# A two-layer decoder trunk: Strassen units copy their first product earlier and place plain pieces later, new costs for the ordering estimate, stores moved to the scalar engine

## The chip, the cores and the metric

The kernel runs on one core of a Trainium2 chip. Its engines are TensorE (PE in the rows; PEld is its weight load), VectorE (DVE), ScalarE (ACT), GpSimd (POOL) and SyncE (SP, which issues DMAs). The metric is the device time of one execution in microseconds (us).

## The reference

`reference()` computes a decoder trunk over 512 tokens of 2048 features. Layer 0 runs an RG-LRU recurrence beside sliding-window attention, layer 1 multi-head latent attention (MLA) beside differential attention. What of it the change touches:

```python
def layer(x):                       # both layers, cut
    z = rmsnorm(x) @ w_in           # one input projection, columns shared out among all branches
    yA, yB = branchA(zA), branchB(zB)
    y = concat(yA * silu(gateA), yB * silu(gateB))
    return x + y @ w_out
# layer 1, branch A: MLA, 8 heads, causal softmax over 512 keys
# layer 1, branch B: differential attention, 8 heads, softmax(q1 k1) - lambda * softmax(q2 k2)
out = rmsnorm(layer1(layer0(x)))
```

## The kernel before

**Products.** Matrices are float32, and a product is made of three products of a reduced type (fp32r): every operand is split into a high half (ACT copies it with rounding) and a low half (DVE subtracts), and PE adds high by high, low by high and high by low. Tiles are named by what they hold: `wr` and `wx` raw weights, `wh` and `wl` their halves, `sh`/`sl`, `yh`/`yl`, `th`/`tl` halves of activations; `mm`, `o`, `sc` and `pt` are the PSUM banks, two of each name.

**Weights.** They come in pieces of 128 x 1024. SP loads a piece, ACT writes its high half and DVE its low one, two pieces ahead of PE (`Piece.want`). There are three slots for the halves: those of piece i may be written only when PE has ended piece i-3. A `Sum` is a piece that DVE first adds up from others.

**Order.** `Plan` is a list scheduler that works while the program is built: the order of PE's, ACT's and DVE's instructions is fixed by its estimates. `pe_cost`, `act_cost` and `dve_cost` say how long an instruction takes, `HOP` is what passes from one engine to another, and generators that `yield after(tile)` go on once the estimate has that tile ready. The order on POOL and SP comes from a scheduler behind it. All instructions are issued through one helper, so that every row of the trace carries its line, L62, and is told by its tiles.

**The two units.** Near the end of layer 1's input projection, `Unit` makes two blocks of 1024 columns in a Strassen-like way: over halves of tokens and features, seven products in place of eight, and sums of products in place of the rest. Its banks are X (`mm`), Y (`o`) and Z (`sc`). X takes the first product (pieces p1), Y and Z the next two (p5, p6); then `first` copies X into two tiles s1 (ACT), and DVE makes s2 = Z + s1 and s3 = Y + s2. The pieces T3_0 to T3_2 go on in X, and the plain pieces P_0 and P_1, products of features outside the scheme, begin anew in Z and Y, which `second` hands over when s3 is planned as done. A T3 or p piece is 12 matmuls of 512 columns, a plain piece 24. The trace shows s1, s2 and s3 as `s`.

```python
def steps(self, name, *ops):          # combine, leave, free: generators, one for each of two banks
    def f():
        for b in range(2):
            for op in ops:
                yield from op(b)
```

**Stores.** When a unit's sums are ready, `away` scales them on ACT and stores them to scratch memory (`vd` and `gd`, eight each); five MLA gates are stored so too (`mgd`). POOL issues these stores.

**End of the layer-1 attention.** Each MLA head makes scores (`sc`), a maximum on DVE with a copy to `p`, an exponential on ACT, a scaling on DVE, transposes on PE (`pt<-p`), a copy on ACT (`aT<-pt`), products with the values on PE (`o<-aT,v`), DVE's product with the gate (`mg<-o,mg`), and the halves `yh` (ACT) and `yl` (DVE), which the output projection reads. Heads run in pairs, and matmuls of the output projection lie between their steps.

Of the kernel before, what the change touches and what calls it, by code (L numbers as in the profile page):

```python
# [15 lines left out]
P = 128  # L16
# [50 lines left out]
def _free(ap):  # L67
    n = 1
    for d in ap.shape[1:]:
        n *= d  # L70
    return n


class Plan:
# [40 lines left out]
    def pe_cost(self, op, args, kw):  # L115
        if op == "transpose":
            return 0.108
        rhs = args[2]
        n = _free(rhs)
        if rhs.dtype == F32R:  # L120
            return 0.003 + (n / 2400.0 if n >= 256 else 0.213)
        return 0.006 + max(n, 64) * 4 / 2400.0

    TABLES = {AF.Exp: "e", AF.Sigmoid: "s", AF.Sqrt: "q", AF.Silu: "u"}

    def act_cost(self, op, args, kw):
        c = 0.1 + _free(args[1]) / 1200.0
        if "accum_out" in kw:
            c += 0.09
        t = self.TABLES.get(args[2])  # L130
        if args[2] == AF.Tanh and self.table not in ("e", "s", "u"):
            t = "s"
        if t and t != self.table:
            self.table = t
            c += 1.3
        return c
# [20 lines left out]
    def after(self, *aps):  # L157

        return max(self.ready.get(a.tensor.name, 0.0) for a in aps)
# [33 lines left out]
def trunk_kernel(ctx: ExitStack, tc, xT, w0, w0o, wg, w1, w1u, wuq, wuk, wuv, w1o, small, cst, outT, outN):  # L193
# [3 lines left out]
    act = Engine(plan, "ACT", nc.scalar, plan.act_cost)  # L197
    dve = Engine(plan, "DVE", nc.vector, plan.dve_cost)
    pool = Engine(plan, "Pool", nc.gpsimd, plan.dma_cost)
    sync = Engine(plan, "SP", nc.sync, plan.dma_cost)  # L200
    after = plan.after
# [17 lines left out]
    def wk(name, dt=F32):  # L219
        return bp.tile([P, S], dt, name=nm(name), tag="w")[:, :]  # L220
# [10 lines left out]
    def bank(tag):  # L231

        t = min(banks[tag])
        banks[tag].remove(t)
        plan.now = max(plan.now, t)
        return ps.tile([P, S], F32, name=nm(tag), tag=tag, bufs=2)[:, :]
# [46 lines left out]
    class Piece:  # L283
# [4 lines left out]
        def __init__(self, src, n, kept=False):  # L288
            self.src, self.n, self.kept = src, n, kept
            self.i = len(pieces)  # L290
            pieces.append(self)
# [150 lines left out]
    def big_job(wt, m, X, done, pre=None, norm=None, kept=(False, False), tag="mm"):  # L442
        return Job(big_parts(wt, m, kept), X, done, pre, norm, tag)
# [92 lines left out]
    first = [bank("o"), bank("o")]  # L536
    W, raws, xin = {}, {}, [None] * KT
# [25 lines left out]
    for k in range(KT):  # L563
# [8 lines left out]
        c = slice((k % 4) * P, (k % 4 + 1) * P)  # L572
# [55 lines left out]
    def evac(acc, norm, name):  # L628
        z = wk(name)
        dve.tensor_tensor(z, acc, norm.r, ALU.mult)  # L630
        return z
# [454 lines left out]
    mgd = dp.tile([8, P, S], F32, name="mgd")[:, :, :]  # L1086
# [3 lines left out]
    def mla_gate_job(h, away):  # L1090
        def done(acc):
            z = evac(acc, n1, "mg")

            def f():
                yield after(z)
                act.activation(z, z, AF.Silu)
                if away:
                    yield after(z)
                    pool.dma_start(mgd[h], z)
                else:  # L1100
                    MG[h] = z
            plan.spawn(f())
        j = big_job(w1, 16 + h, X1, done, None, n1)
        if h == 0:
            j.pre = lambda: plan.spawn(differences())
# [5 lines left out]
    def differences():  # L1111

        A, B = slice(0, 256), slice(256, 512)

        def fetch(k):
            xa, xb = wk("xa"), wk("xb")
            sync.dma_start(xa, x1d[k])
            sync.dma_start(xb, x1d[8 + k])
            return xa, xb

        nxt = fetch(0)
        for k in range(NT):
            xa, xb = nxt
            if k + 1 < NT:
                nxt = fetch(k + 1)
            yield after(xa, xb)
            act.activation(xa, xa, AF.Identity, scale=col(C_G1 + k))
            act.activation(xb, xb, AF.Identity, scale=col(C_G1 + 8 + k))
            yield after(xa, xb)
            t13, t42 = wk("ta"), wk("tb")  # L1130
            dve.tensor_tensor(t13[:, A], xa[:, A], xa[:, B], ALU.subtract)
            dve.tensor_tensor(t42[:, A], xb[:, A], xb[:, B], ALU.subtract)
            dve.tensor_tensor(t13[:, B], xa[:, B], xb[:, B], ALU.subtract)
            dve.tensor_tensor(t42[:, A], t42[:, A], t13[:, A], ALU.subtract)
            dve.scalar_tensor_tensor(t42[:, B], t13[:, A], -1.0, xb[:, B], ALU.mult, ALU.subtract)
            yield after(t42)
            r = []
            for t in (t13, t42):
                h = wk("th", F32R)
                high(h, t)  # L1140
                r.append(h)
            yield after(*r)
            for i, t in enumerate((t13, t42)):
                l = wk("tl", F32R)
                low(l, t, r[i])
                r[i] = r[i], l
            TS[k] = r

    class Unit:
# [3 lines left out]
        def __init__(self, wt, sink):  # L1153
            self.wt, self.sink, self.pre = wt, sink, None
            W = lambda m, kh, i: wt[m, kh, i]
            n = NT // 2
            seq = []
            self.keep = []
            for i in range(n):
                p1 = Sum([W(0, 0, i)])  # L1160
                p5 = Sum([W(1, 0, i), W(1, 1, i)], wide=False)
                p6 = Sum([], (p5, p1), None)
                self.keep.append(p6)
                seq += [(p1, "X", "B11", i), (p5, "Y", "T1", i), (p6, "Z", "T2", i)]
            seq.append(self.first)
            for i in range(n):
                seq.append((Sum([W(0, 0, i), W(1, 0, i)], (), 1), "X", "T3", i))
                if i < 2:
                    if i == 0:
                        seq.append(self.second)  # L1170
                    seq.append((Piece(W(0, i, 3), 1024), "ZY", None, i))
            seq.append(self.third)
            for i in range(n):
                p2 = Sum([W(0, 1, i)])
                p3 = Sum([], (self.keep[i], p2), 0)
                seq += [(p2, "Z", "B21", i), (p3, "Y", "B22", i)]
            seq.append(self.fourth)
            for i in range(n):
                seq.append((Sum([W(1, 1, i)], (), 0, i % 2 == 0), "X", "T4", i))
            seq.append(self.fifth)  # L1180
            for i in range(2):
                seq.append((Piece(W(1, i, 3), 1024), "XZ", None, i))
            self.seq = seq
            jobs.append(self)
# [84 lines left out]
                yield plan.now  # L1269
            return f  # L1270

        def first(self):
            def copy(b):
                p = self.banks["X"][b]
                yield after(p)
                self.vals["s1"][b] = wk("s1")
                act.activation(self.vals["s1"][b], p, AF.Copy)
            self.steps("s1", copy)
            self.wait("s1")
            self.begun -= {("X", 0), ("X", 1)}  # L1280
            self.steps("s3", self.combine("s2", "Z", "s1", False), self.combine("s3", "Y", "s2", False))
# [22 lines left out]
    def away(dst, func):  # L1304

        def sink(m, n, z):
            yield after(z)
            act.activation(z, z, func, scale=n1.col[:, n : n + 1])
            yield after(z)
            pool.dma_start(dst[4 * m : 4 * m + 4].rearrange("h p t -> p h t")[:, :, n * P : (n + 1) * P],  # L1310
                           z.rearrange("p (h t) -> p h t", h=4))
        return sink

# [477 lines left out]
```

## Time and profile before

| what | value |
|---|---|
| time, median of 3 runs | 1546.92 us (1546.2 to 1547.11) |
| the profiled execution's own time | 1546.05 us |
| its span, first to last instruction | 1544.1 us |
| granted TensorE clock | 0.999 |
| PE busy | 1531.9 us, 99% of the span |
| PEld busy | 1282.4 us, 83% |
| DVE busy | 932.0 us, 60% |
| ACT busy | 730.9 us, 47% |
| POOL busy | 71.1 us, 5% |

The busy share of PE counts overlapping matmuls as one stretch. A short wait of PE is seen as a distance between the starts of two matmuls that is longer than in an undisturbed stretch.

### The profile page before, as it was taken

Reading aid. Unit: us, or ns where it says so; the run is one execution under the profiler, and the core shown is the slowest. Engines: PE = TensorE matmul, PEld = TensorE weight load, DVE = VectorE, ACT = ScalarE, POOL = GpSimd, SP = SyncE. Lnnn points to the kernel's source line nnn. Section 1 sums busy time; section 2 is a strip of 40 time slices with the busy share of each in tenths; the row PEclk is TensorE's granted clock in tenths of the full one; section 3 lists DMA queues with packets and bytes.
Section 4 is the critical chain, followed back from the end, with each engine's and each line's share of the span. In section 5 each row is a group of like instructions: output and inputs, shape, how many; then the busy total and the mean of one; then the engine's idle time right before and its main releaser. Section 6 shows DMA issues by size and latency. Waiting matters only on the chain.

```text
span 1544.1 us, 19513 instructions
## 1 busy us (share of the span) xinstructions
PE 1531.9 (99%) x7376; PEld 1282.4 (83%) x7376; DVE 932.0 (60%) x1726; ACT 730.9 (47%) x1289; POOL 71.1 (5%) x118
## 2 busy tenths in 40 slices
PE   9999999999999999999999999999999999999997
PEld 7888888888888888878888888888888888888887
DVE  7877676677863434675764677666344476743343
ACT  7465465555652333534433556555333456632222
POOL 0000000000000100000002000000000000010000
PEclk9999999999999999999999999999999999999999
DMA  7223222222244444645636322322232321343323
GB/s 285 86 86 92 90 85 86 87 81 82 94 132 136 150 139 159 220 165 171 211 124 210 96 89 83 96 83 78 87 96 89 96 79 59 116 144 96 98 94 110
DMA packets 58494, 179.74 MB, mean 116 GB/s; under 512 B 7056, under 2 KB 9248, under 8 KB 58272
## 3 DMA queue, kind: packets, MB, share of 16 engines
q1 hardware_dynamic: 50784, 153.84, 31.4%
q0 software_dynamic: 7616, 24.66, 4.8%
q8 instruction: 58, 0.95, 0.3%
q14 instruction: 36, 0.29, 0.1%
HBM read 164.58 MB, written 13.89 MB: 116 GB/s over the span
## 4 chain that ended last, share of the span: by engine, by line
PE 96%; issue 2%; DVE 1%; DMA 0%; ACT 0%; SPq 0%; POOLq 0%; DVEq 0%; POOL 0%; ACTq 0%
PE mm L62 78%; PE sc L62 8%; PE o L62 7%; PE pt L62 3%; DMA xin<-in_xT 0%; ACT wh L62 0%; DVE s L62 0%; SPq L62 0%; DVE wl L62 0%; DVE so L62 0%; DVE sl L62 0%; DVE mg L62 0%; DVE wx L62 0%; POOLq L1786 0%; ACT sh L62 0%
## 5 line engine op out<-in xcount | busy, mean ns | idle before, releaser
L62 DVE TENSOR_TENSOR wl<-wr,wh 128x1024 fp32r<-128x1024 f32 (+1 forms) x236 | 280.7, 1190 | 379.2 <-ACT wh L62 375.8
L62 PE MATMUL mm<-sh,wh 128*128 128x512 f32 x1056 | 419.4, 397 | 0.0
L62 ACT ACTIVATE wh<-wr 128x1024 fp32r<-128x1024 f32 (+1 forms) x236 | 243.8, 1033 | 361.3 <-PE mm L62 252.7
L62 PE MATMUL mm<-sl,wh 128*128 128x512 f32 x1056 | 412.1, 390 | 0.0
L62 PE MATMUL mm<-sh,wl 128*128 128x512 f32 x1056 | 412.1, 390 | 0.0
L62 PEld LDWEIGHTS mm<-sh,wl 128*128 128x128 f32 x1056 | 198.2, 188 | 42.6
L62 PEld LDWEIGHTS mm<-sh,wh 128*128 128x128 f32 x1056 | 198.5, 188 | 36.3
L62 PEld LDWEIGHTS mm<-sl,wh 128*128 128x128 f32 x1056 | 198.8, 188 | 35.5
L62 PE MATMUL mm<-yh,wh 128*128 128x512 f32 x448 | 174.9, 390 | 0.0
L62 PE MATMUL mm<-yl,wh 128*128 128x512 f32 x448 | 174.4, 389 | 0.0
L62 PE MATMUL mm<-yh,wl 128*128 128x512 f32 x448 | 174.4, 389 | 0.0
L62 PEld LDWEIGHTS mm<-yl,wh 128*128 128x128 f32 x448 | 84.1, 188 | 17.5 <-DVE yl L62 0.3
L62 PEld LDWEIGHTS mm<-yh,wl 128*128 128x128 f32 x448 | 84.1, 188 | 17.5
L62 PEld LDWEIGHTS mm<-yh,wh 128*128 128x128 f32 x448 | 84.1, 188 | 17.1
L62 ACT ACTIVATE p<-p,negm 128x128 f32<-128x128 f32 (+3 forms) x96 | 53.8, 560 | 59.9 <-DVE negm L62 58.2
L62 DVE CUSTOM_DVE_ANT_0 p<-sc,cc 128x128 f32<-128x128 f32 (+3 forms) x96 | 46.7, 487 | 41.2 <-PE sc L62 40.7
L62 ACT ACT_TABLE_LOAD x36 | 46.2, 1283 | 1.4 <-PEq L1781 0.7
L62 ACT ACTIVATE sq<-xr 128x512 f32<-128x512 f32 (+1 forms) x33 | 19.3, 586 | 55.0 <-DVE xr L62 55.0
L62 ACT ACTIVATE aT<-pt 128x128 f32<-128x128 f32 (+3 forms) x64 | 27.5, 434 | 37.0 <-PE pt L62 36.5
L62 DVE TENSOR_TENSOR ss<-ss,sq 128x512 f32<-128x512 f32 (+1 forms) x54 | 36.1, 668 | 10.3 <-ACT sq L62 9.4
L62 PE MATMUL mm<-ch,wh 128*128 128x512 f32 x104 | 41.6, 400 | 0.0
L62 PE MATMUL mm<-cl,wh 128*128 128x512 f32 x104 | 40.6, 391 | 0.0
(332 smaller groups left out, 2385.2 us busy)
## 6 DMA issues: line engine op xcount, KB each, us to landing
wr<-in_w SPq DMA_DIRECT2D x134, 512.0 KB, 3.5
wr<-in_w0o SPq DMA_DIRECT2D x32, 512.0 KB, 3.6
wr<-in_w1o SPq DMA_DIRECT2D x32, 512.0 KB, 3.5
wr<-in_w1u SPq DMA_DIRECT2D x30, 512.0 KB, 3.7
wx<-in_w1u SPq DMA_DIRECT2D x40, 256.0 KB, 4.7
wr<-in_wuq SPq DMA_DIRECT2D x12, 384.0 KB, 3.1
xin<-in_xT SPq DMA_DIRECT2D x16, 256.0 KB, 5.2
xr<-in_xT POOLq DMA_DIRECT2D x16, 256.0 KB, 3.9
```

The costliest lines, as they stand in the source:

```text
L62: return f(*args, **kw)
```

## The change

It has three parts. The estimates of `Plan` get other numbers: an fp32r matmul n x 17/38400 us and at least 0.108, an fp32 one less of a constant, an ACT instruction 0.2 + n/1230, a DMA that ACT issues 0.06. The stores of gates and units are issued by ACT, where the row before them is ACT's own. In a unit the copy s1 is planned when the last p1 piece has been placed, ahead of p5 and p6, and P_0 and P_1 stand one T3 piece later: T3_0, T3_1, P_0, T3_2, P_1, where it was T3_0, P_0, T3_1, P_1, T3_2.

```diff
@@ -118,13 +118,15 @@
         rhs = args[2]
         n = _free(rhs)
         if rhs.dtype == F32R:
-            return 0.003 + (n / 2400.0 if n >= 256 else 0.213)
-        return 0.006 + max(n, 64) * 4 / 2400.0
+            return max(0.108, n * 17 / 38400.0)
+        return 0.002 + max(n, 64) * 4 / 2400.0
     TABLES = {AF.Exp: "e", AF.Sigmoid: "s", AF.Sqrt: "q", AF.Silu: "u"}
     def act_cost(self, op, args, kw):
-        c = 0.1 + _free(args[1]) / 1200.0
+        if op == "dma_start":
+            return 0.06
+        c = 0.2 + _free(args[1]) / 1230.0
         if "accum_out" in kw:
             c += 0.09
         t = self.TABLES.get(args[2])
@@ -1095,8 +1097,7 @@
                 yield after(z)
                 act.activation(z, z, AF.Silu)
                 if away:
-                    yield after(z)
-                    pool.dma_start(mgd[h], z)
+                    act.dma_start(mgd[h], z)
                 else:
                     MG[h] = z
             plan.spawn(f())
@@ -1161,14 +1162,14 @@
                 p5 = Sum([W(1, 0, i), W(1, 1, i)], wide=False)
                 p6 = Sum([], (p5, p1), None)
                 self.keep.append(p6)
-                seq += [(p1, "X", "B11", i), (p5, "Y", "T1", i), (p6, "Z", "T2", i)]
+                seq += [(p1, "X", "B11", i)] + [self.zeroth] * (i == n - 1) + [(p5, "Y", "T1", i), (p6, "Z", "T2", i)]
             seq.append(self.first)
             for i in range(n):
                 seq.append((Sum([W(0, 0, i), W(1, 0, i)], (), 1), "X", "T3", i))
-                if i < 2:
-                    if i == 0:
+                if i > 0:
+                    if i == 1:
                         seq.append(self.second)
-                    seq.append((Piece(W(0, i, 3), 1024), "ZY", None, i))
+                    seq.append((Piece(W(0, i - 1, 3), 1024), "ZY", None, i - 1))
             seq.append(self.third)
             for i in range(n):
                 p2 = Sum([W(0, 1, i)])
@@ -1269,13 +1270,15 @@
                 yield plan.now
             return f
-        def first(self):
+        def zeroth(self):
             def copy(b):
                 p = self.banks["X"][b]
                 yield after(p)
                 self.vals["s1"][b] = wk("s1")
                 act.activation(self.vals["s1"][b], p, AF.Copy)
             self.steps("s1", copy)
+
+        def first(self):
             self.wait("s1")
             self.begun -= {("X", 0), ("X", 1)}
             self.steps("s3", self.combine("s2", "Z", "s1", False), self.combine("s3", "Y", "s2", False))
@@ -1306,8 +1309,7 @@
         def sink(m, n, z):
             yield after(z)
             act.activation(z, z, func, scale=n1.col[:, n : n + 1])
-            yield after(z)
-            pool.dma_start(dst[4 * m : 4 * m + 4].rearrange("h p t -> p h t")[:, :, n * P : (n + 1) * P],
+            act.dma_start(dst[4 * m : 4 * m + 4].rearrange("h p t -> p h t")[:, :, n * P : (n + 1) * P],
                            z.rearrange("p (h t) -> p h t", h=4))
         return sink
```

The numbers of instructions on PE, DVE and SP stay as they are. ACT has 21 DMAs and 3 table loads more, POOL 21 DMAs fewer.

DVE around the first unit's sums, before the change (`wl` is a low half, here of T3_1 and at the end of P_1, `s1` to `s3` the sums, `wx` the raw weights that are added up):

```order
L62 TENSOR_TENSOR wl_1109_5769<-wx_1091_5690,wh_1108_5768 128x512
L62 TENSOR_TENSOR wl_1109_5769<-wx_1092_5691,wh_1108_5768 128x512
L62 TENSOR_TENSOR s2_1110_5780<-sc_1070_5592,s1_1105_5760 128x512
L62 TENSOR_TENSOR s3_1111_5788<-o_1065_5571,s2_1110_5780 128x512
L62 TENSOR_TENSOR s2_1112_5790<-sc_1071_5593,s1_1106_5762 128x512
L62 TENSOR_TENSOR s3_1113_5792<-o_1066_5572,s2_1112_5790 128x512
L62 TENSOR_TENSOR wl_1115_5796<-wr_1097_5716,wh_1114_5794 128x1024
```

The same place now:

```order
L62 TENSOR_TENSOR wl_1109_5772<-wr_1092_5692,wh_1108_5770 128x1024
L62 TENSOR_TENSOR s2_1110_5780<-sc_1070_5592,s1_1102_5736 128x512
L62 TENSOR_TENSOR wx_1098_5718<-wr_1097_5716,wx_1098_5718 128x512
L62 TENSOR_TENSOR wx_1099_5719<-wr_1097_5716,wx_1099_5719 128x512
L62 TENSOR_TENSOR wl_1112_5791<-wx_1098_5718,wh_1111_5790 128x512
L62 TENSOR_TENSOR wl_1112_5791<-wx_1099_5719,wh_1111_5790 128x512
L62 TENSOR_TENSOR s3_1113_5808<-o_1065_5572,s2_1110_5780 128x512
L62 TENSOR_TENSOR s2_1114_5810<-sc_1071_5593,s1_1103_5738 128x512
L62 TENSOR_TENSOR s3_1115_5812<-o_1066_5573,s2_1114_5810 128x512
```

Before, the four sums stand together between the low halves of T3_1 and that of P_1. Now P_0's low half stands ahead of s2 of bank 0, and four instructions that make T3_2 (two sums of raw weights, two low halves) stand between that s2 and the other three sums.

PE at the end of the layer-1 attention, before (`pt<-p` are transposes of probabilities, `o<-aT,v` products with the values, `mm<-yh` and `mm<-yl` the output projection, `x4` a run of four):

```order
L62 MATMUL pt_2382_11612<-cc_2_78,p_2369_11544 128x128 x4
L62 MATMUL pt_2383_11617<-cc_2_78,p_2374_11557 128x128 x4
L62 MATMUL mm_2353_11479<-yh_2329_11398,sh_2321_11379 128x512
L62 MATMUL mm_2353_11479<-yl_2330_11399,sh_2321_11379 128x512
L62 MATMUL mm_2353_11479<-yh_2329_11398,sl_2322_11380 128x512
L62 MATMUL o_2323_11386<-aT_2384_11622,v_2154_10761 128x128
L62 MATMUL o_2323_11386<-aT_2384_11622,v_2165_10810 128x128
L62 MATMUL o_2323_11386<-aT_2384_11622,v_2173_10858 128x128
L62 MATMUL o_2323_11386<-aT_2384_11622,v_2181_10896 128x128
L62 MATMUL o_2337_11427<-aT_2385_11627,v_2154_10761 128x128
```

The same place now:

```order
L62 MATMUL mm_2297_11282<-yl_2383_11617,sh_2283_11232 128x512
L62 MATMUL mm_2297_11282<-yh_2382_11616,sl_2284_11233 128x512
L62 MATMUL pt_2384_11626<-cc_2_78,p_2373_11567 128x128 x3
L62 MATMUL o_2343_11451<-aT_2385_11630,v_2154_10760 128x128
L62 MATMUL o_2343_11451<-aT_2385_11630,v_2164_10807 128x128
L62 MATMUL o_2343_11451<-aT_2385_11630,v_2171_10853 128x128
L62 MATMUL pt_2386_11637<-cc_2_78,p_2381_11610 128x128 x4
L62 MATMUL o_2343_11451<-aT_2387_11642,v_2154_10760 128x128
L62 MATMUL o_2343_11451<-aT_2387_11642,v_2164_10807 128x128
L62 MATMUL o_2343_11451<-aT_2387_11642,v_2171_10853 128x128
L62 MATMUL o_2343_11451<-aT_2387_11642,v_2181_10894 128x128
L62 MATMUL mm_2297_11282<-yh_2388_11649,sh_2283_11232 128x512
```

Before, the last two heads' transposes stand together, three matmuls of the output projection follow, and then the value products of both heads. Now the last head (o_2343) has its last two blocks of queries one after the other: transposes, value products, transposes, value products, the product with the gate's halves, with no other matmul between.

## Rows read from the trace of the kernel before

**Rows 1.** The page, part 1: busy time, share of the span, instructions.

```profile
PE 1531.9 (99%) x7376; PEld 1282.4 (83%) x7376; DVE 932.0 (60%) x1726; ACT 730.9 (47%) x1289; POOL 71.1 (5%) x118
```

**Rows 2.** The chain that ended last: start us, us, what; one undisturbed piece of it.

```profile
430.58 184.41 PE mm L62 x813
```

**Rows 3.** Waits of PE: us in total, times, longest us.

```profile
PE sc L62 <- DVE s L62: 1.3, 4, 0.4
```

**Rows 4.** Timeline, first unit: start us, us, engine, line, operation [idle before <-releaser].

```profile
688.55 1.29 DVE L62 TENSOR_TENSOR wx<-wr,wx 128x512 f32<-128x512 f32 x2
...
688.79 0.39 PE L62 MATMUL mm<-wh,th 128*128 128x512 f32 x1
...
689.35 1.16 ACT L62 ACTIVATE wh<-wx 128x512 fp32r<-128x512 f32 x2 [1.00 <-DVE wx L62]
...
690.02 1.29 DVE L62 TENSOR_TENSOR wl<-wx,wh 128x512 fp32r<-128x512 f32 x2 [0.18 <-ACT wh L62]
...
691.28 0.39 PE L62 MATMUL mm<-wh,tl 128*128 128x512 f32 x1
691.75 1.06 ACT L62 ACTIVATE wh<-wr 128x1024 fp32r<-128x1024 f32 x1 [1.25 <-issue]
691.95 0.69 DVE L62 TENSOR_TENSOR s<-o,s 128x512 f32<-128x512 f32 x1
...
691.97 0.50 PE L62 MATMUL sc<-wh,sh 128*128 128x512 f32 x1 [0.30 <-DVE s L62]
...
692.56 0.68 DVE L62 TENSOR_TENSOR s<-sc,s 128x512 f32<-128x512 f32 x1
...
693.29 0.50 PE L62 MATMUL sc<-wh,sh 128*128 128x512 f32 x1 [0.36 <-DVE s L62]
...
693.88 1.22 DVE L62 TENSOR_TENSOR wl<-wr,wh 128x1024 fp32r<-128x1024 f32 x1
```

**Rows 5.** Timeline, end of the layer-1 attention.

```profile
1361.67 0.69 DVE L62 CUSTOM_DVE_ANT_0 p<-sc,cc 128x512 f32<-128x512 f32 x1 [0.37 <-PE sc L62]
...
1367.63 1.04 PE L62 MATMUL pt<-cc,p 128*128 128x128 f32 x8
1368.33 1.09 ACT L62 ACTIVATE aT<-pt 128x512 f32<-128x512 f32 x2 [3.35 <-PE pt L62]
...
1368.43 0.48 PE L62 MATMUL mm<-yh,sh 128*128 128x512 f32 x1
...
1369.20 1.95 PE L62 MATMUL o<-aT,v 128*128 128x128 f32 x16
1370.29 0.69 DVE L62 TENSOR_TENSOR mg<-o,mg 128x512 f32<-128x512 f32 x1 [3.24 <-PE o L62]
...
1370.90 0.47 PE L62 MATMUL mm<-yh,sh 128*128 128x512 f32 x1
...
1371.08 0.63 ACT L62 ACTIVATE yh<-mg 128x512 fp32r<-128x512 f32 x1 [1.66 <-DVE mg L62]
...
1371.79 0.68 DVE L62 TENSOR_TENSOR yl<-mg,yh 128x512 fp32r<-128x512 f32 x1
...
1372.53 0.50 PE L62 MATMUL mm<-yl,sh 128*128 128x512 f32 x1 [0.26 <-DVE yl L62]
...
1372.87 0.40 PE L62 MATMUL mm<-yh,sl 128*128 128x512 f32 x1
...
1373.94 0.39 PE L62 MATMUL mm<-yh,sh 128*128 128x512 f32 x1
```

**Rows 6.** Timeline, first unit's stores and the second last piece's halves.

```profile
730.26 3.00 POOL L62 DMA_DIRECT2D vd<-s  x4 [62.26 <-ACT s L62]
...
731.72 1.04 ACT L62 ACTIVATE wh<-wr 128x1024 fp32r<-128x1024 f32 x1
...
738.98 0.39 PE L62 MATMUL mm<-wh,sh 128*128 128x512 f32 x1
```

**Rows 7.** Costliest groups of ACT: busy us, mean ns | idle us before, releasers.

```profile
L62 ACT ACT_TABLE_LOAD x36 | 46.2, 1283 | 1.4 <-PEq L1781 0.7
```

## Prediction

> **What bounds the kernel now.** I read the busy shares first. PE is busy for 1531.9 us, 99% of the span, and every other engine is far below [rows 1]. A matmul's row overlaps the next one, so that share hides short waits; I take the distance between starts for the real price. The chain that ended last shows it in a stretch where PE waits for nothing: 813 matmuls of 512 columns in 184.41 us, 0.2268 us each [rows 2]. Against that distance the timeline shows where PE loses time, and a change of order can touch only such places, or make new ones.
>
> The Trainium skill, "Perfetto Trace Analysis", section "Identifying the Most-Contended Engine", holds that the busy share of matmuls is a poor measure of headroom, and names the share of weight loads as a better one. By it the 83% of PEld would leave up to 17% of the span, an estimate of some 262 us. The trace disagrees with that reading here: the undisturbed stretch has the same distance of 0.2268 us throughout, so that the unused part of the load is no time that an order could win.
>
> The waits that I use below are two. In each unit PE waits for sums on DVE [rows 3], four times in the two units. In the first unit, the start at 691.28 is followed by four starts, the last at 693.29: 2.01 us, where four distances are 0.91; the first start after a wait is also followed late by 0.11 (the restart of rows 5 took 0.34: from 1372.53 to 1372.87), which adds 0.11 behind the second wait. That is 1.2 us a unit, 2.4 in all [rows 4]. At the end of the layer-1 attention, nine distances from 1370.90 to 1373.94 take 3.04 us where they should take 2.04: 1.0 us [rows 5].
>
> **The units: 0 (from -2.4 to +0.4).** The edit places P_0 one T3 piece later, so PE reaches its first bank at 688.79 + 24 x 0.2268 = 694.23, where it was 691.51. If s2 and s3 were made when they are now, nothing would be waited for, and 2.4 us would go. But the order of DVE changes too. I follow it with the row durations. P_0's halves may be written when the piece three before it has ended, which is now p6_2, at 688.79. ACT followed such an end by 0.24 (691.28 + 0.23 = 691.51, then 691.75) and took 1.06, the low half took 1.22 and ends about 0.1 + 1.22 behind: 688.79 + 0.24 + 1.06 + 0.08 + 1.22 = 691.39. Then comes s2 of bank 0, to 692.0 (the sums start 0.61 apart: 691.95, 692.56). Then T3_2: two sums of weights, whose high halves start 0.80 behind the first sum's start and whose low halves 0.67 behind that (688.55, 689.35, 690.02), so they start at 692.0 + 1.47 = 693.47 and, two of them in 1.29, end at 694.7. Then s3 of bank 0 to 695.3, and s2 of bank 1 to 695.3 + 0.68 = 696.0. PE has started P_0 in bank 0 of Z at 694.23 and reaches bank 1 three matmuls later, at 694.91; it gets it 0.05 behind the sum's end (692.56 + 0.68, then 693.29), at 696.04: a wait of 1.1, and 1.2 with the restart. That is what the two waits cost now. The second unit has the same order of rows. The wait moves from the piece's first two banks to the second; I take 0, with the whole 2.4 as the gain if DVE is ahead of this sum, and +0.4 if its rows stand apart by their full length (0.68 and 1.29) instead of by their starts. The copy s1, planned earlier, goes before these sums on an engine that is not waited for here, and costs nothing; if s1 were late, s2 of bank 0 would be, whose slack is over 2 us (692.0 against 694.23).
>
> **The end of the layer-1 attention: +4.0 (3.3 to 4.5).** Now the last two heads end side by side: eight transposes, three matmuls of the projection while ACT copies, eight value products (two rows of the trace each), and then nine matmuls around the gate's halves. The new cost numbers move one head back by a block, and the last of it has nothing between its steps. From the end of the last scores on:
> - Three matmuls, then `mm<-yh,sh`, then one that needs yl. PE reaches that at 4 x 0.2268 = 0.91. DVE has the maximum of those scores ahead of yl: 0.24 to its start (the first four value products end at half of 1369.20 to 1370.90, 1370.05; DVE starts at 1370.29), 0.69 (1361.67), 0.68 for yl (1371.79), 0.06 to PE (1371.79 + 0.68, then 1372.53): 1.67, a wait of 0.76.
> - Three transposes, then value products that need their copy: 0.30 from PE to ACT (eight transposes of 0.10 from 1367.63 to 1368.43, of which the first four end at 1368.03; 1368.33), 0.55 for the copy (1.09 for two), 0.06 to PE: 0.91. It comes twice, as the second transposes stand behind the first value products: 1.82.
> - The last value product, then `mg` after 0.24, 0.69, `yh` after 0.10, 0.63, 0.06 to PE: 1.72. Then yl: it follows yh by 0.08 and takes 0.68 and 0.06, less the distance of the matmul between (0.23), less what of yh's end was passed on already (0.06) and the 0.11 of that restart: 0.42.
> - Three of these restarts are not hidden in a longer wait: 0.33.
> Together 0.76 + 1.82 + 1.72 + 0.42 + 0.33 = 5.05, less the 1.0 that goes: +4.0. All durations are [rows 5]. The lower bound has the first wait hidden, the upper one a full 0.11 restart behind each of the five waits and a queue of 0.3 on ACT or DVE.
>
> **Sliding-window heads: +0.2 (0 to 1.4).** In two heads of layer 0 the last scores stand 24 matmuls ahead of the transposes that need them, not 27. Three distances are 0.68; the trace of before shows no wait there, so some of it is slack.
>
> **The stores: 0 (0 to +1.2).** POOL took 0.75 us for each issue, four in 3.00; on ACT I have no row. The closest place is the end of the first unit, where four stores now stand before the high half of the second last piece: that started at 731.72 and took 1.04, the low half takes 1.22 and PE needs it at 738.98 [rows 4, 6]. So 738.98 - 731.72 - 1.04 - 1.22 = 5.0 us cover them, and 3.0 is less. If the issue held ACT for twice as long, 6.0, the excess of 1.0 would be waited for.
>
> **Table loads: 0 (0 to +3.8).** The new order has three more, of 1.28 us [rows 7], all in layer 0. ACT is idle for half of the span [rows 1], and none of the three stands ahead of a tile that PE takes next; without that cover they would be 3 x 1.28 = 3.8.
>
> **Elsewhere: 0 (-0.5 to +1.5).** The rest of PE's order has the same work in nearly the same places. The last transposed gain in the tail stands three matmuls of 128 columns earlier, which slack takes up.
>
> **The sum.** 0 + 4.0 + 0.2 + 0 + 0 + 0 = +4.2. On the profiled execution's 1546.05 (its span of 1544.1 and 1.95 around it) this is 1550.25. That execution is 0.87 below the median, so the median's own time would be **1551.1 us**, 0.27% slower.
>
> **The rivals.**
> 1. *The units' waits go.* DVE makes s2 and s3 before T3_2's sums delay them, if its raw weights come late or the low half of P_0 ends earlier than 691.39. It decides when over 1.1 of the 2.4 us go: then the total is within 0.2%. All gone: 1551.1 - 2.4 = 1548.7. For it speaks that PE comes 2.7 us later to the piece; against it, that DVE's order is fixed and the chain from 688.79 has no gap to shorten.
> 2. *The attention's end is no longer than now*, which is the case on the other side. Its waits would have to sum to 1.0 again: the scalar engine copies and the DVE's product would have to be hidden by matmuls. Then 1551.1 - 4.0 = 1547.1, no change. It decides when the five waits sum to under 3.9. Against it: no other matmul stands between these steps.
> 3. *A store holds ACT until it lands, or a chain that the new costs tightened is late*: the four stores of 4 to 5 us each would be 18 us, far over the 5.0 of cover. 13 us of wait would be 1564; a small case, two or three waits of 1 us, is 1553 to 1554.
> 4. *The new estimate wins in layer 0.* Its order may drop small waits that I did not find; from half of the units' 2.4 and the attention's end at its lower bound the total would be 1551.1 - 1.2 - 0.7 = 1549.2. It needs 5.4 us more for a gain.
>
> **How the numbers follow.** I give the forecast 0.55, the first rival 0.17, the second 0.12, the third 0.11, the fourth 0.05. Two per mille of the median, 3.1 us, is about what a measurement of this kernel can tell from no change: same lies between 1543.8 and 1550.0. The forecast's own range, 1549.5 to 1553.5, is nearly all slower (0.50 of 0.55); the third rival is slower, the first two are the same, the fourth is half faster, half the same. So slower is 0.61, same 0.36, faster 0.03. The range from 1547.6 to 1553.6 leaves out half of the second rival, the large case of the third, and the fourth.
>
> **What would show it.** Right for the units: P_0's first matmul in the second Z bank about 1.1 late, and DVE with T3_2's low halves ahead of s3 of bank 0. Right for the attention's end: waits of PE for `yl`, `aT` twice, `yh` and `yl` behind the last scores, together near 5 us. For the stores: ACT's issues of 0.1 to 0.8 us, and the high half at the unit's end no more than 3 us later. For the rest: no new wait of PE over 0.3 us. The prediction is wrong if the median is below 1550, or if these waits are there and PE's time elsewhere has shrunk.

## The result and the profile after

The changed kernel takes 1554.32 us (median of 4 runs, 1553.08 to 1555.12), the one before 1546.63 (4 runs): a ratio of 1.005, 95% interval 1.0035 to 1.0065. It is slower, as forecast, but by 7.7 us and not by the 4.5 or so of the prediction (1551.1), and outside the range (to 1553.6).

The profiled execution took 1555.09 us, 9.04 more than that of before. The page's first part hardly tells the two apart. Only PE differs: the same 7376 matmuls are busy for 4.1 us more, and it is idle for 1553.2 - 1536.0 = 17.2 us, 12.2 before:

```profile
PE 1536.0 (99%) x7376; PEld 1284.9 (83%) x7376; DVE 932.5 (60%) x1726; ACT 735.6 (47%) x1292; POOL 56.7 (4%) x97
```

The waits of PE (us in total, times, longest) show what came, beside [rows 3]:

```profile
PE mm L62 <- DVE yl L62: 1.9, 4, 0.8
PE sc L62 <- DVE s L62: 1.6, 2, 0.8
PE mm L62 <- ACT yh L62: 1.4, 1, 1.4
PE o L62 <- ACT aT L62: 1.3, 2, 0.7
...
PE sc L62 <- DVE xl L62: 0.3, 1, 0.3
```

The units' four waits for `s` have become two longer ones. The waits for `yh` and `aT` and two of those for `yl` are the attention's end; the other two for `yl`, the longest among them, are at the end of layer 0, where the prediction had none.

**The unit.** The timeline of the first unit, beside [rows 4]:

```profile
692.22 0.39 PE L62 MATMUL mm<-wh,th 128*128 128x512 f32 x1
...
692.46 1.06 ACT L62 ACTIVATE wh<-wr 128x1024 fp32r<-128x1024 f32 x1 [1.09 <-issue]
693.56 1.23 DVE L62 TENSOR_TENSOR wl<-wr,wh 128x1024 fp32r<-128x1024 f32 x1 [1.38 <-ACT wh L62]
694.70 0.69 DVE L62 TENSOR_TENSOR s<-sc,s 128x512 f32<-128x512 f32 x1
695.30 1.29 DVE L62 TENSOR_TENSOR wx<-wr,wx 128x512 f32<-128x512 f32 x2
...
696.76 1.29 DVE L62 TENSOR_TENSOR wl<-wx,wh 128x512 fp32r<-128x512 f32 x2 [0.17 <-ACT wh L62]
697.65 0.39 PE L62 MATMUL sc<-wh,sh 128*128 128x512 f32 x1
...
697.97 0.68 DVE L62 TENSOR_TENSOR s<-o,s 128x512 f32<-128x512 f32 x1
698.11 0.39 PE L62 MATMUL sc<-wh,sl 128*128 128x512 f32 x1
698.57 0.68 DVE L62 TENSOR_TENSOR s<-sc,s 128x512 f32<-128x512 f32 x1
...
699.31 0.50 PE L62 MATMUL sc<-wh,sh 128*128 128x512 f32 x1 [0.81 <-DVE s L62]
```

P_0 starts at 697.65 without a wait; its fourth matmul, in the second Z bank, starts 1.20 behind its third where 0.23 is due. DVE's two sums and two low halves of T3_2 stand between the first s2 and the second. The prediction's chain starts where PE begins T3_0, here 692.22, 3.43 us later than before. Shifted by that much, it gave 692.46 for the high half, 694.82 for the low half's end, 698.7 for the second s2 and 699.47 for PE; the rows have 692.46, 694.79, 698.57 and 699.31.

**The attention's end**, beside [rows 5]:

```profile
1372.18 0.69 DVE L62 CUSTOM_DVE_ANT_0 p<-sc,cc 128x512 f32<-128x512 f32 x1 [0.91 <-PE sc L62]
...
1373.54 0.50 PE L62 MATMUL mm<-yl,sh 128*128 128x512 f32 x1 [0.47 <-DVE yl L62]
...
1374.15 0.52 PE L62 MATMUL pt<-cc,p 128*128 128x128 f32 x3
1374.71 0.49 ACT L62 ACTIVATE aT<-pt 128x384 f32<-128x384 f32 x1 [0.93 <-PE pt L62]
1375.26 0.94 PE L62 MATMUL o<-aT,v 128*128 128x128 f32 x6 [0.58 <-ACT aT L62]
1376.03 0.60 PE L62 MATMUL pt<-cc,p 128*128 128x128 f32 x4
1376.67 0.60 ACT L62 ACTIVATE aT<-pt 128x512 f32<-128x512 f32 x1 [1.46 <-PE pt L62]
1377.32 1.16 PE L62 MATMUL o<-aT,v 128*128 128x128 f32 x8 [0.69 <-ACT aT L62]
...
1379.92 0.50 PE L62 MATMUL mm<-yh,sh 128*128 128x512 f32 x1 [1.45 <-ACT yh L62]
1380.65 0.50 PE L62 MATMUL mm<-yl,sh 128*128 128x512 f32 x1 [0.23 <-DVE yl L62]
...
1381.98 0.63 PE L62 MATMUL mm<-yh,sh 128*128 128x512 f32 x1
1382.40 0.63 PE L62 MATMUL mm<-yl,sh 128*128 128x512 f32 x1
```

All five waits that were forecast are there. What was not forecast is in the last two rows: nothing is waited for, and yet the matmuls are 0.42 apart. The table by windows (length, PE, PEld, DVE, ACT and POOL busy, granted clock) says why:

```profile
1372.00:1378.00 6.00, 4.27 (x26) 2.98 (x25) 2.35 (x7) 1.90 (x4) 0.57 (x2) 1.00 0.28 87
1378.00:1382.00 4.00, 2.33 (x12) 1.57 (x11) 1.98 (x3) 0.63 (x1) 0.54 (x1) 0.97 0.25 66
1382.00:1385.00 3.00, 3.00 (x9) 2.33 (x8) 1.30 (x3) 1.57 (x2) 0.00 (x0) 0.50 0.00 0
1385.00:1390.00 5.00, 5.00 (x23) 4.16 (x22) 1.32 (x3) 0.63 (x1) 0.54 (x1) 0.98 0.49 157
```

Behind two stretches in which PE idles for 3.4 of 10 us, the granted clock is 0.50, the lower level of 1.2 GHz, for some 3 us.

**The end of layer 0**, where the kernel before waits for nothing:

```profile
443.00 0.39 PE L62 MATMUL mm<-yh,wh 128*128 128x512 f32 x1
443.13 0.68 DVE L62 TENSOR_TENSOR yl<-gz,yh 128x512 fp32r<-128x512 f32 x1
443.73 1.22 DVE L62 TENSOR_TENSOR wl<-wr,wh 128x1024 fp32r<-128x1024 f32 x1
443.87 0.50 PE L62 MATMUL mm<-yl,wh 128*128 128x512 f32 x1 [0.48 <-DVE yl L62]
...
444.44 0.39 PE L62 MATMUL mm<-yh,wh 128*128 128x512 f32 x1
444.87 2.49 DVE L62 TENSOR_TENSOR yl<-gz,yh 128x512 fp32r<-128x512 f32 x4
...
445.61 0.50 PE L62 MATMUL mm<-yl,wh 128*128 128x512 f32 x1 [0.78 <-DVE yl L62]
```

The output projection catches up with the last branches: it waits for a low half, and again for the next, which stands behind a weight's low half on DVE.

### The profile page after: what moved, and what is told of

Same layout as the page of the kernel before. It is cut to its first block, busy times and chain, and to the rows that moved or that the text cites. A ratio compares the mean times of both kernels' runs of the same rounds, so it can differ in the third digit from the quotient of the medians.

```text
span 1553.2 us, 19487 instructions
## 1 busy us (share of the span) xinstructions
PE 1536.0 (99%) x7376; PEld 1284.9 (83%) x7376; DVE 932.5 (60%) x1726; ACT 735.6 (47%) x1292; POOL 56.7 (4%) x97
## 4 chain that ended last, share of the span: by engine, by line
PE 68%; issue 1%; DVE 1%; ACT 0%; POOLq 0%; POOL 0%; DVEq 0%; ACTq 0%
PE mm L62 55%; PE sc L62 6%; PE o L62 6%; PE pt L62 2%; DVE s L62 0%; ACT wh L62 0%; DVE wl L62 0%; DVE so L62 0%; DVE mg L62 0%; DVE yl L62 0%; DVE wx L62 0%; ACT aT L62 0%; POOLq L1788 0%; POOL rcf L62 0%; DVE p L62 0%
## 5 line engine op out<-in xcount | busy, mean ns | idle before, releaser
L62 PEld LDWEIGHTS mm<-yh,wh 128*128 128x128 f32 x448 | 84.3, 188 | 17.2
L62 ACT ACTIVATE aT<-pt 128x384 f32<-128x384 f32 (+3 forms) x64 | 27.2, 432 | 35.9 <-PE pt L62 35.4
L62 ACT ACTIVATE pr<-pr,negm 128x128 f32<-128x128 f32 (+1 forms) x64 | 30.4, 475 | 28.3 <-DVE negm L62 28.3
```

The lines of the kernel that those rows point to most:

```text
L62: return f(*args, **kw)
```

## The experiments

Each ran in five rounds beside the kernel before. "Before" here is 1546.18 us with e1 to e4, 1546.04 with e5 to e8, 1546.16 with e9 to e11.

**e1, the costs alone.** Kernel before, with

```diff
-            return 0.003 + (n / 2400.0 if n >= 256 else 0.213)
-        return 0.006 + max(n, 64) * 4 / 2400.0
+            return max(0.108, n * 17 / 38400.0)
+        return 0.002 + max(n, 64) * 4 / 2400.0
...
-        c = 0.1 + _free(args[1]) / 1200.0
+        c = 0.2 + _free(args[1]) / 1230.0
```

> The kernel before with the new cost numbers alone (matmul and ACT costs); units and stores as before. Theory (the new order makes all of the loss): 1554.3 us, within 1.2; waits of PE at the end of the layer-1 attention of 5 us and more, the low clock level behind them, two waits for yl at the end of layer 0 of 0.6 and 0.9 us; the units wait as before, 1.2 us each. Rival (the stores on ACT disturb the weight loads and the end of layer 0): at most 1551 us, which is the forecast of the order alone, and no wait at the end of layer 0.

Measured: 1554.97 us, ratio 1.0055 (1.0042 to 1.0067). Its profile has the waits at the ends of both layers and the low clock. The cost numbers make the whole loss.

**e2, the unit's edits alone** (`zeroth`, and the plain pieces one T3 piece later, as in the diff above).

> The kernel before with the edits of the unit alone (copy s1 earlier, plain pieces one T3 piece later); costs and stores as before. Theory (the wait moves to the second Z bank): 1546.4 us, within 0.5, with one wait of about 1 us in each unit. Rival (the units gain, and the new costs eat it): 1544.2 us, no wait in the units over 0.3 us.

Measured: 1546.05 us, ratio 0.9996 (0.9987 to 1.0005), and one wait in each unit:

```profile
PE sc L62 <- DVE s L62: 1.6, 2, 0.8
```

The wait moved. No change, as the prediction had it.

**e3, the stores alone** (`pool.dma_start` becomes `act.dma_start` in `mla_gate_job` and `away`, with a cost of 0.06).

> The kernel before with the 21 stores issued by ACT alone; the order of PE and DVE is that of before, row by row. Theory (their issue is covered): 1546.6 us, within 0.5. Rival (ACT is held by the issue, or the loads of SP by the other queue): 1548 us and more, with new waits of PE near 720 to 820 us.

Measured: 1546.55 us, ratio 1.0003 (0.9994 to 1.0012), no new wait of PE. The stores cost nothing. In the changed kernel's trace one issue takes ACT's queue 0.37 to 0.41 us, half of POOL's 0.75 [rows 6].

**e4, the units with DVE's order mended.** e2, with the four sums placed together:

```diff
-            self.steps("s3", self.combine("s2", "Z", "s1", False), self.combine("s3", "Y", "s2", False))
+            self.steps("s3", self.four)
+
+        def four(self, b):
+            if b == 0:
+                yield after(*self.banks["Z"], *self.vals["s1"], *self.banks["Y"])
+                for out, x, y in (("s2", "Z", "s1"), ("s3", "Y", "s2")):
+                    for k in range(2):
+                        r = wk(out)
+                        dve.tensor_tensor(r, self.banks[x][k], self.vals[y][k], ALU.add)
+                        self.vals[out][k] = r
+            else:
+                yield after(*self.vals["s3"])
```

> The kernel of e2 with the four sums s2, s2, s3, s3 placed on DVE in one piece as soon as the Z banks are ready, ahead of T3_2's weights. Theory (DVE's order around T3_2 keeps the units' wait): no wait in the units over 0.3 us and 1544.3 us, 2.3 below before. Rival (T3_2's halves come late in turn, or the waits in the units are not what PE's time goes by): 1546.4 us, as e2.

Measured: 1543.65 us, ratio 0.9984 (0.9975 to 0.9992), faster than both kernels. DVE's rows in the first unit:

```profile
692.22 1.22 DVE L62 TENSOR_TENSOR wl<-wr,wh 128x1024 fp32r<-128x1024 f32 x1 [1.66 <-ACT wh L62]
693.36 1.28 DVE L62 TENSOR_TENSOR s<-sc,s 128x512 f32<-128x512 f32 x2
694.56 1.28 DVE L62 TENSOR_TENSOR s<-o,s 128x512 f32<-128x512 f32 x2
695.75 1.28 DVE L62 TENSOR_TENSOR wx<-wr,wx 128x512 f32<-128x512 f32 x2
```

The four sums now precede T3_2's, and no wait for `s` is left. So the later place of the plain piece, with the sums made in one piece, is worth 2.4 us (e2 less e4), and the order on DVE had taken all of it. `combine` yields until s2 is ready before it places s3 on the same engine; in that time the planner comes to the next piece and places its four instructions first.

**e5 and e6, the costs in one layer.** The changed kernel with a flag `new` in `Plan`: new numbers where it is set, old ones elsewhere. It changes behind the last product of layer 0 (set until there in e5, from there on in e6). Both keep the edits of units and stores.

```diff
     for i, j in enumerate(jobs):
+        if i == jobs.index(O0.jobs[-1]) + 1:
+            plan.new = False
         if j is O1.jobs[0]:
```

> The changed kernel with the new cost numbers only up to layer 0's last product, and the old ones from there on; its order is that of the changed kernel to there, row by row, and that of before with the unit and store edits behind it. Theory (layer 0 loses some 3.5 us, by waits that were costed at 0 or 0.2): 1549.6 us, within 0.8. Rival (layer 0 loses as forecast, 0.2, and the rest comes from a disturbance of the whole run): 1546.5 us.

> The reverse of e5: old numbers in layer 0, new ones behind it. Theory (the attention's end loses 4.0 by its waits, and 1.5 more by the low clock level behind them): 1551.5 us, within 1. Rival (the forecast's 4.0 alone, the clock's fall being something that the run brings along): 1550.2 us. e5 and e6 should sum to the loss of the changed kernel, 8 us.

Measured: e5 1549.68 us (1.0024, 1.0015 to 1.0033), e6 1551.33 (1.0036, 1.0024 to 1.0049). That is 3.6 and 5.3 us, together 8.9; the changed kernel has 7.7 by its medians and 9.0 by its profiled execution. Layer 0 loses 3.6 where 0.2 was forecast, and the rest 5.3 where 4.0 was.

**e7 and e9, the waits filled.** To the changed kernel (e7) and to e6 (e9) products of constants are added, in the last head alone:

```diff
             yield from transposed(p, n, aT)
+            if h == 7 and n >= 2:
+                for _ in range(3):
+                    nc.tensor.matmul(o[:, n * P : (n + 1) * P], cc[:, 0:P], cc[:, P : 2 * P], start=True, stop=True,
+                                     skip_group_check=True)
...
+        if h == 7:
+            idle = []
+            yield from take("pt", idle)
+            for _ in range(6):
+                nc.tensor.matmul(idle[0][:, :P], cc[:, 0:P], cc[:, P : 2 * P], start=True, stop=True, skip_group_check=True)
+            banks["pt"].append(plan.now + 2.0)
         yield after(o)
```

> The changed kernel with twelve products more on PE, of constants, into banks that are overwritten or not read: three ahead of each of the last head's two value products that wait for a copy, six behind its last; the order of everything else is the same. Theory (the clock falls because PE idles through these waits): no stretch at the low level behind them, 1.4 us less than the changed kernel, 1553 us. Rival (the clock's fall has another cause): the low level stays, 1554.5 us or more, as the added products take nothing from the waits. If the products are longer than the waits the time is higher by what they run over, at most 0.3 us.

> The kernel of e6 with the twelve products of constants of e7 in the last head's waits, all else in the same order. The products take about what the waits took, so the waits themselves are worth nothing here. Theory (the clock falls where PE idles): no stretch at the low level behind the attention, and 1.1 us less than e6, 1550.2 us. Rival (the level falls with no regard to what PE does there, and e7's profile merely missed it): 1551.3 us as e6, with the low stretch.

Measured: e7 1554.3 us (1.0052, 1.004 to 1.0065), e9 1550.17 (1.0026, 1.0015 to 1.0037). The granted clock is full behind the attention in both; e6 and e9 by windows, in this order:

```profile
1374.00:1378.00 4.00, 2.56 (x10) 1.73 (x10) 1.39 (x2) 0.63 (x1) 0.54 (x1) 0.75 0.23 66
1378.00:1382.00 4.00, 4.00 (x16) 3.24 (x15) 2.19 (x3) 1.58 (x2) 0.00 (x0) 0.82 0.00 0
```

```profile
1374.00:1378.00 4.00, 3.65 (x28) 2.95 (x26) 1.39 (x2) 1.21 (x2) 0.54 (x1) 1.00 0.22 66
1378.00:1382.00 4.00, 4.00 (x18) 3.29 (x19) 1.56 (x2) 1.58 (x2) 0.00 (x0) 1.00 0.00 0
```

e9 is 1.2 us below e6, the 1.1 expected, although it does more work on PE, and six of its seven runs are below the fastest of e6. The starts in the two profiles place the gain. From the last head's scores to the first product of the next weight, e6 and then e9 have:

```profile
1366.93 0.47 PE L62 MATMUL sc<-mh,mh 128*128 128x512 f32 x1
...
1380.66 0.40 PE L62 MATMUL mm<-yh,wh 128*128 128x512 f32 x1
```

```profile
1368.06 0.47 PE L62 MATMUL sc<-mh,mh 128*128 128x512 f32 x1
...
1380.61 0.39 PE L62 MATMUL mm<-yh,wh 128*128 128x512 f32 x1
```

That is 13.73 us in e6 and 12.55 in e9, and all of the difference lies behind the wait for `yh`: up to its end both take 9.18. In the changed kernel the same stretch takes 13.80, in e7 12.54. So the clock falls because PE idles.

e7's time misses its expectation of 1553. Its profile shows another low stretch near the start, where PE waits for its first operands, and so does that of e9 (below it):

```profile
8.00:12.00 4.00, 3.72 (x9) 2.83 (x10) 2.58 (x4) 2.80 (x6) 0.00 (x0) 0.57 1.05 406
```

```profile
8.00:12.00 4.00, 4.00 (x11) 2.95 (x12) 2.63 (x5) 2.57 (x5) 0.00 (x0) 0.57 1.05 404
```

By the starts, each of the two is 1.0 us behind its counterpart from 18 us on. That takes back most of the gain in these two executions: e9's took 1550.9 us, e6's 1550.99. The added products are no cause of it, as they come long after, and a slow start is not theirs alone: in e4's profile PE's rows at 8 to 13 us are 0.63 us long as well, and that execution, 1545.71 us, is 2.1 above e4's median. How the unprofiled runs of e7 began is not known; their mean clocks, 0.999 at 1553.52 and 1553.97 us and 0.997 at 1554.3 and 1554.56, fit two that were without it. So e7's time decides nothing, and e9 and the starts carry the point.

**e8 and e11, one number each**: the new matmul costs alone, and the new ACT costs alone, each in the kernel before.

> The kernel before with the new matmul costs alone. Its order has six matmuls of the projection between the last head's transposes and their value products, so by the durations of the trace two of the five waits at the attention's end go. Theory (the loss comes from where fillers are left over, not from a number being wrong): the waits at the attention's end are 2 to 3 us and the time is 1547.5 to 1551. Rival (the matmul number itself brings the loss): 1553 us or more.

> The kernel before with the new ACT costs alone. Its order has the last MLA head alone at the end as well, with three matmuls of the projection between its second transposes and their value products. Theory (an order by any of the new numbers ends unluckily where fillers run out): waits at the attention's end of 3 to 4 us, 2 to 3 more than before, and with the clock's fall up to 4; with layer 0, of which I say nothing but 0 to 3.5, 1548 to 1553 us. Rival (the matmul number makes the loss, the ACT number is harmless): 1546.5 us, within 0.7.

Measured: e8 1551.88 us (1.0035, 1.0023 to 1.0048), e11 1551.55 (1.0037, 1.0025 to 1.005). Both lose, and neither in the way of the other. e8 has only two waits behind the last head, as its order let expect, but the low clock behind them, and its time is above the 1551 that I gave. e11's time and its waits at the attention's end are as expected, but its largest wait is at the end of layer 0:

```profile
PE mm L62 <- DVE yl L62: 3.0, 3, 2.0
```

So no single number is the culprit. Each set of numbers gives another order, and of the four tried (both, one, the other, none) the old one happens to run out of cover least.

**e10, new costs in six of layer 0's eight tiles.** e5, with the flag cleared eight jobs ahead of the output projection: `if i == jobs.index(O0.jobs[0]) - 8`.

> The kernel of e5 with the new numbers only for the first six of layer 0's eight tiles, the old ones from there on. Theory (some 1.6 of layer 0's 3.5 us come from the last sliding-window head ending late before the output projection, which the last two tiles' order decides): the two waits for yl of 0.6 and 0.9 us are gone or below 0.3, and 1548.1 us. Rival (they follow from what the first six tiles leave behind): both waits stay, 1549.6 us as e5.

Measured: 1547.81 us, ratio 1.0012 (1.0003 to 1.0021). The waits for `yl` at the end of layer 0 are gone; the one that is left is the old one at the attention's end:

```profile
PE mm L62 <- DVE yl L62: 0.3, 1, 0.3
```

e5 to e10 is 3.64 - 1.65 = 2.0 us for the order of the last two tiles and the output projection, the end of layer 0; the first six tiles keep 1.65. The guess that the last value product's place decides was too simple, though: e10 has it as near the first `yl` as e5, eight rows of PE's order, where before has 17. What e10 undoes is the order of the last tiles' work on DVE and ACT as a whole. Where the time goes is seen on DVE, in e5 and then e10:

```profile
436.35 1.22 DVE L62 TENSOR_TENSOR wl<-wr,wh 128x1024 fp32r<-128x1024 f32 x1 [1.84 <-ACT wh L62]
...
438.09 1.70 DVE L62 TENSOR_TENSOR so<-so,o 64x256 f32<-64x256 f32 x4
```

```profile
434.38 1.71 DVE L62 TENSOR_TENSOR so<-so,o 64x256 f32<-64x256 f32 x4
```

In e5 DVE stands idle for 1.84 us for a weight, with four sums of value products (`so`) behind it in its order; in e10 these fill the gap, and the last `yl` come earlier. That this alone does it was not tried.

## Why the prediction was wrong

Its sign and its main term hold. One step was not made, one term was put at nothing and was not, and one was too small. By steps:

- **The units: 0.** Right, with its chain of rows (e2: -0.1, e4: the mechanism). The first rival is refuted for this change, and e4 is the case that it described.
- **The attention's end: +4.0.** The waits are right. By starts of PE, with what the matmuls between would take by themselves: 0.64 (1372.67 to 1373.54) for `yl`, 0.79 and 0.86 for the two copies, 1.75 for `yh`, 0.50 for the last `yl`, and 0.35 of restarts: 4.9, less the old 1.0 is +3.9. **The step that failed here is one that was not made**: what PE's idling does to its clock. Behind these waits eight distances at the low level cost 1.5 us in the profiled execution (from 1381.66 to 1384.96, 3.30 where 1.81 is due), 1.2 by e9 against e6. The second rival is refuted: the waits sum to 4.9, not to under 3.9.
- **Sliding-window heads: +0.2.** Too small, though inside its range: in the changed kernel's trace a value product of three heads, not two, is late by 0.25 with its restart (behind 248.40, 298.86 and 349.32), 0.75 in all. e10's +1.65 for the first six tiles is more than heads. By starts 1.3 of it can be found: two such heads (0.49), a late start at a head's scores (0.35, behind 379.34) and a wait for `xl` in the recurrence's gate products that is no head's (0.43, behind 152.18).
- **Elsewhere: 0.** **This is the step that failed in full.** "The rest of PE's order has the same work in nearly the same places" was not so at the end of layer 0, which lost 2.0 (e5 less e10), beyond the bound of 1.5. By starts of the changed kernel, 1.8 went at its two waits for `yl`, and 0.76 more at gate products (0.42 behind 152.45, 0.34 behind 380.38). The prediction followed late chains at one end, that of layer 1, and not at the other, where a branch hands over to an output projection in the same way. The fourth rival, a gain in layer 0, is refuted by e5.
- **Stores and table loads: 0.** Right for the stores (e3). The table loads were not tried alone; e1 has them and shows no wait of PE that begins at one.

Sum by runs: 0 + 3.9 + 1.2 + 1.65 + 2.0 = 8.75, against 8.9 for e5 and e6 together and 7.7 for the medians of the changed kernel. The third rival, with a chance of 0.11, had named beside the stores a chain that the new costs tightened, for 1553 to 1554 us; that is what was added to the forecast, and it did not need the stores.

## What to carry to other kernels

More exact numbers in a list scheduler do not mean a better order. The new ones are nearer to the rows: 0.2267 us for a matmul of 512 columns where the distance is 0.2268 (0.2163 before), and 1.03 us for ACT's 1024 columns where the rows have 1.04 to 1.06 (0.95 before). All three new sets lost 5 to 9 us, so compare the orders they yield, at every place where branches end and the filler work runs out. Where a consumer is moved later to hide a wait, check that the producer's engine has not been given work ahead of what is waited for; here four instructions undid 2.4 us. And a chain of short waits on TensorE costs more than their sum when the clock falls behind it, here 1.2 to 1.5 us more.

## What the runs showed of the hardware

The granted clock fell to 0.50 behind PE's idling at the attention's end, for about 3 us, and only after PE had taken up full work again: it was still 1.00 from 1372 to 1378 with PE busy for 4.27 of 6 us. The Trainium skill, "TensorE: Matmul & The Clock Gate", section "A second HAM failure mode: psum-queue depth-cycling", tells of a kernel whose clock goes down and up because PE idles often and briefly between groups of matmuls; the trace agrees in that no wait here is longer than 1.75 us, and has one fall behind them, not a series.

It does not fall every time, and does not go by the sum of the waits. e11 has waits of 0.74, 0.21, 1.61 and 0.50 us there and its profile shows no low stretch; e8's has one behind 1.67 and 0.50. Of e8's five runs two have a mean clock of 0.999 (1550.37 and 1550.88 us) and three 0.997 (1551.88 to 1552.57), on average 1.6 us apart. The same spread of two groups is in the changed kernel's four runs, 1553.08 and 1553.55 against 1555.09 and 1555.12. Both fit the fall's price, but a mean clock does not say where in the run it fell, and those of the changed kernel are too alike (0.998 and 0.997), so neither shows it.
